# Loads on ACT's queue, one row of shifts and another order of the last heads, in a one-core hybrid decoder step

## The chip, the core and the metric

The kernel runs on one core of a Trainium2 chip. The core has five engines that run on their own and wait for one another through semaphores: TensorE (PE) multiplies matrices into PSUM, VectorE (DVE), ScalarE (ACT) and GpSimd (POOL) work on rows, and SyncE (SP) here only issues transfers (DMAs). ACT and POOL can issue transfers too. The metric is the device time of one execution in microseconds; lower is better.

## What is computed

One layer of a decoder for a prompt of 2048 positions and for 8 decode rows of one position each, with 512 cached positions per row. All data is float32.

- `h = rms_norm(x)`, then one product `p = h @ w_in` (1024 to 3592 columns), split into q, k, v, the forget gate, `za`, `u`, `gv`, `zc`.
- Attention, 8 heads of 64: q and k are RMS-normed, the logit of query t and key s is `q.k * SCALE + c_t - c_s` with `c` the running sum of `log_sigmoid(fz + b_f)`, under a causal mask; then softmax and the sum over v.
- A gating group: `gv` normed, multiplied inside chunks of 128 positions by a lower triangular matrix, plus a bias, times `u`.
- `y = x + concat(attn * silu(za), mix * u * silu(zc)) @ w_out`. Keys, values, log gates and the normed `gv` of the decode rows are outputs too.

The decode rows do the same with keys, values and gates gathered from pages of a cache by `page_table`.

## The kernel before

For precision each factor is split into two parts that TensorE takes at full rate, so a product is three matmuls (hi x hi, hi x lo, lo x hi).

**Order.** TensorE's instructions stay in the order in which the program writes them. The other engines' are ordered by a planner, which simulates the time line and takes what is ready first. The kernel keeps its own clock of TensorE's work (`Pe.clock`, from a number of nanoseconds given with each matmul). `later(ns, fn)` puts a piece of work off until that clock has moved on by `ns`; what it then writes may not be planned ahead of the last matmul written. `pump()` runs what is due. At the end of the program each instruction on SP in the attention stage is tied in the same way to the last matmul written before it. Instructions that ACT issues are not part of that last tie.

**Stage 1** (to about 590 us): `order` runs through eight units of columns of `w_in`. For units 3, 0, 1, 2 (q, k, v, gate) and 4 (`gv`) each of the 16 tiles of 128 positions is one product of 24 matmuls into a bank `acc` (four banks). Units 5, 6 and 7 (`u`, `zc`, `za`) work with features on the partitions and do only the first two chunks of 512 positions (`cp` 0 and 1); the rest is left as filler. `sample_products` multiplies the decode rows with a unit's weights; it joins tile 14 (`NT - 2`), or the last group of `cp` 1. Weights are loaded by `load_unit` (L291) and split by ACT or POOL and by DVE (L253 to L256). From tile 8 of unit 4 on, `decode_scores` loads the cached keys, 32 pages of 256 KB.

**Stage 2** (to about 1175 us): attention. `UNITS` lists 32 units (head, chunk of 512 queries), a unit of chunk c having 4c+4 key tiles. `values` does for each key tile two score matmuls into a bank `sc` (three banks), an exponential on ACT (L991) into one of ten ring tiles, and the row sums' addition on POOL (L1000); the sums over v (`av`) run after each eight key tiles. Two key tiles `k1` (hi and lo) and `k2` (hi and rows for gates and shifts) and the values `vst` belong to a head; `load_keys` and `load_values` load them on SP (L852, L853; L861, L862, L864). `load_queries` (L882 to L886) loads the next unit's queries in five transfers, `QLEAD` = 6 key tiles before the unit's end.

The exponential needs a shift per query, so `maxima` computes all scores once more, some 0.8 heads ahead, with DVE reducing each bank (`tp`, three banks) to a minimum (L925, L927). `shifts` turns four columns of minima into two rows (hi and lo, L942, L943), which are transposed, copied by ACT (L949) and stored to `mrow` (L953); `load_queries` brings them back as rows 66 and 67 of the queries.

After a unit its weighted values `at` (L1012 to L1014) are stored to `aT`, the reciprocal row sums (L1021 to L1031) to `rT`. After an odd head `gate` loads both heads' rows, `z` and the sums (L1080 to L1083), multiplies them and stores to `gm`. When the last pair of heads has finished a chunk, its four tiles can go through the output product: `out_inputs` loads a tile (L1101, L1102), ACT and DVE split it, `out_products` multiplies by `w_out`, whose sixteen blocks `load_out_weights` brings (L1067).

**Fillers.** `fill(ns)` writes matmuls of the remaining `u`, `zc`, `za` work, then of the output product, into the gaps, at `FILL` = 0.5 of the attention's own clock (0.95 in the last three units). What is left of the output product runs alone at the end (stage 3). `decode_attention` runs beside the attention from head 1 on: gates summed by one scan (L684), then for each of 8 rows four pages of cached values into a tile `vb` (L643), a product and a store.

**Places.** Large tiles (8 KB a partition) share 16 places: normed rows of both remaining chunks 8, ring tiles 2, `k1` and `k2`, `keep`, `vb`, later output weights. Small ones (`s2`, 2 KB a partition) share 11.

Of the kernel before, what the change touches and what calls it, by code (L numbers as in the profile page):

```python
# [9 lines left out]
F32 = mybir.dt.float32  # L10
F32R = mybir.dt.float32r
# [8 lines left out]
P = 128  # L20
# [4 lines left out]
NH = 8  # L25
# [37 lines left out]
WOENG = ('act',)  # L63
# [15 lines left out]
def hymba_step(ctx, tc, x_prompt, x_sample, cache_k, cache_v, cache_logf, page_table, g_norm, w_in,  # L79
# [45 lines left out]
    def s2(dt=F32, t="s2"):  # L125
        return wk.tile([P, 512], dt, tag="t2", name=tname(t))

# [102 lines left out]
    mrow = dr.tile([NH, 2, SEQ], F32, name="mrow")  # L230
# [436 lines left out]
    def decode_attention():  # L667
# [16 lines left out]
        nc.vector.tensor_tensor_scan(cc, one, lfT, 0.0, op0=ALU.mult, op1=ALU.add)  # L684
# [23 lines left out]
        for b in range(B):  # L708
            hs = slice(b * NH, (b + 1) * NH)
            vb = s8(t="vb").rearrange("p (g f) -> p g f", g=NPG)  # L710
            page_loads(b, range(NPG), [(cv, lambda g: vb[:, g])])
# [12 lines left out]
            yield DEC[2]  # L724
# [122 lines left out]

    def load_keys(h):

        k2 = s8(F32R, "k2")  # L850
        b = 512 + h * HD
        nc.sync.dma_start(k2[:HD].bitcast(F32), qk_hi[b:b + HD])  # L852
        nc.sync.dma_start(k2[HD:HD + 4].bitcast(F32), kx[h])  # L853
        return dict(h=h, k2=k2)

    def load_values(hd):
# [17 lines left out]
    def load_queries(h, c):  # L874
# [11 lines left out]
        nc.sync.dma_start(t[HD + 2:HD + 4, 512:].bitcast(F32), mrow[h, :, cs])  # L886
# [10 lines left out]
    def maxima(hd):  # L897

        h = hd["h"]
        nxt = qhi.pop() if qhi else load_hi(h, 0)  # L900
        for c in range(2):
            q = nxt
            for i in range(8 * c, 8 * c + 8, 2):
                if i == 2:
                    nxt = load_hi(h, 1)
                if i == 10 and h + 1 < NH:
                    qhi.append(load_hi(h + 1, 0))
                if i % 4 == 0:
                    part = sm.tile([P, 4, i // 4 + 1], F32, tag="mn", bufs=3, name=tname("mn"))
                cuts = [pieces((j + 1) * P) for j in (i, i + 1)]  # L910
                ends = []
                for j, cut in zip((i, i + 1), (cuts[0], cuts[1][::-1])):
                    for (c0, m) in cut:
                        n = cuts[j - i].index((c0, m))
                        end = n == len(cut) - 1
                        sp = bank("tp")[:, :m]
                        mm(sp, q[:HD + 2, (j % 8) * P:(j % 8 + 1) * P], hd["k2"][:HD + 2, c0:c0 + m], True, not end,
                           max(m, 256) * 0.422)
                        if end:
                            ends.append((sp, m, j, n))  # L920
                            if j > i:
                                for (sp, m_, _, _) in ends:
                                    mm(sp[:, m_ - P:], identb, maskb[:, 0], False, True, 56)
                                for (sp, _, j_, n_) in ends:
                                    nc.vector.tensor_reduce(part[:, j_ % 4, n_:n_ + 1], sp, axis=AX.X, op=ALU.min)  # L925
                        else:
                            nc.vector.tensor_reduce(part[:, j % 4, n:n + 1], sp, axis=AX.X, op=ALU.min)  # L927
                        yield m * 0.422
                if i % 4 == 2:
                    shifts(h, i // 4, part)  # L930
# [404 lines left out]
```

## Time and profile before

| | |
|---|---|
| median of 3 runs (lowest to highest) | 1345.62 us (1344.01 to 1347.55) |
| the profiled execution's own time | 1351.46 us |
| its span | 1349.7 us |
| PE busy in the span | 1304.4 us, 97% |
| DVE / POOL / ACT busy | 675.7 / 618.0 / 443.2 us |
| bytes moved | 183.10 MB |
| mean granted TensorE clock | 0.983 |

Busy time counts instructions being worked on; waiting, and the issue of transfers, is not busy. A granted clock of 1.00 is full speed. A wait row names the engine and line that waited, what ended the wait, the total, the count and the longest. A timeline row has start and duration in us, engine, line, operation, output and inputs, and in brackets the idle time before it and what ended that. `SPq` is SP's queue issuing a transfer.

### The profile page before, as it was taken

How to read it: one execution, taken by the hardware profiler on the slowest of the kernel's cores; microseconds unless marked ns; L12 is line 12 of the kernel's file. 1: busy time of each engine (PE TensorE's matmuls, PEld its weight loads, DVE VectorE, ACT ScalarE, POOL GpSimd, SP SyncE). 2: the span in 40 equal slices, each digit the busy share in tenths (PEclk: the TensorE clock that was granted, in tenths of full speed). 3: DMA queues.
4: the chain of work that ended last, by engine and by line, in shares of the span. 5: the costliest groups of instructions: out<-in, count | busy, mean ns of one | idle time of the engine just before them, and what ended most of it. 6: DMA issues, size and time to landing. Idle time of an engine off the chain costs nothing.

```text
span 1349.7 us, 19517 instructions
## 1 busy us (share of the span) xinstructions
PE 1304.4 (97%) x6544; PEld 1012.9 (75%) x6544; DVE 675.7 (50%) x1280; ACT 443.2 (33%) x805; POOL 618.0 (46%) x703
## 2 busy tenths in 40 slices
PE   6999999999999999999999999999999998999998
PEld 5999999999887877866666566656656664688877
DVE  4346654534678454264486453454455675222321
ACT  5542332322222111114454343534454455310000
POOL 3113343423223464317777666686769668600000
PEclk9999999999999999989999899998999998999999
DMA  6644354545113655534343845466374745573321
GB/s 216 187 120 111 86 141 120 156 133 158 51 50 106 190 176 156 159 81 127 77 116 112 190 124 140 133 176 177 91 201 113 189 126 174 167 245 116 108 76 50
DMA packets 170807, 183.10 MB, mean 136 GB/s; under 512 B 39403, under 2 KB 125867, under 8 KB 169139
## 3 DMA queue, kind: packets, MB, share of 16 engines
q1 hardware_dynamic: 166818, 173.08, 46.5%
q10 hardware_dynamic: 3488, 8.39, 1.6%
q8 instruction: 52, 0.85, 0.3%
q14 instruction: 49, 0.39, 0.1%
q0 software_dynamic: 400, 0.38, 0.1%
HBM read 121.53 MB, written 60.28 MB: 135 GB/s over the span
## 4 chain that ended last, share of the span: by engine, by line
PE 86%; DMA 5%; DVE 4%; issue 2%; SPq 2%; ACT 1%; POOL 0%; DVEq 0%; ACTq 0%; POOLq 0%
PE acc L174 35%; PE sc L174 21%; PE fl L174 10%; PE av L174 8%; PE tp L174 6%; PE tp L178 4%; DMA q<-qk_hi 2%; PE pm L174 1%; DMA xp<-in_x_prompt_dram 1%; DVE wl L256 1%; DVE mn L925 1%; DMA vb<-in_cache_v_dram 1%; DMA kb<-in_cache_k_dram 1%; SPq L641 0%; SPq L291 0%
## 5 line engine op out<-in xcount | busy, mean ns | idle before, releaser
L1000 POOL TENSOR_TENSOR acc<-acc,p 128x512 f32<-128x512 f32 (+3 forms) x256 | 284.9, 1113 | 61.8 <-ACT p L991 48.4
L991 ACT ACTIVATE p<-sc,zero 128x512 f32<-128x512 f32 (+1 forms) x320 | 194.9, 623 | 179.9 <-PE sc L174 175.0
L174 PE MATMUL acc<-wh,hh 128*128 128x384 f32 (+2 forms) x640 | 228.8, 357 | 0.0
L174 PE MATMUL acc<-wl,hh 128*128 128x384 f32 (+2 forms) x640 | 222.8, 348 | 0.8 <-DVE wl L256 0.8
L174 PE MATMUL acc<-wh,hl 128*128 128x384 f32 (+2 forms) x640 | 222.5, 348 | 0.6 <-DVE hl L248 0.6
L174 PE MATMUL sc<-q,k 128*128 128x512 f32 (+7 forms) x640 | 202.7, 398 | 11.9 <-DMA q<-qk_hi 10.5
L174 PE MATMUL sc<-wo,am 128*128 128x512 f32 x720 | 164.3, 390 | 0.0
L174 PEld LDWEIGHTS sc<-wo,am 128*128 128x128 f32 x720 | 134.9, 188 | 28.2
L927 DVE TENSOR_REDUCE mn<-tp 128x1 f32<-128x320 f32 (+5 forms) x192 | 118.4, 631 | 59.4 <-PE tp L174 58.0
L174 PEld LDWEIGHTS sc<-q,k 128*128 128x128 f32 (+1 forms) x640 | 120.0, 197 | 31.9 <-issue 13.8
L174 PE MATMUL av<-p,vst 128*64 128x512 f32 (+3 forms) x640 | 136.6, 547 | 0.0
L236 POOL TENSOR_SCALAR sm<-sm 128x6 f32<-128x6 f32 (+3 forms) x84 | 20.7, 246 | 238.5 <-DVE sm L389 170.5
L174 PE MATMUL tp<-k,q 66*128 66x384 f32 (+6 forms) x320 | 122.6, 398 | 6.2 <-DVE mn L925 2.4
L174 PEld LDWEIGHTS acc<-wh,hh 128*128 128x128 f32 x640 | 120.6, 188 | 7.4 <-POOL wh L255 0.3
L174 PEld LDWEIGHTS acc<-wl,hh 128*128 128x128 f32 x640 | 120.7, 189 | 6.2 <-DVE wl L256 1.6
L174 PEld LDWEIGHTS acc<-wh,hl 128*128 128x128 f32 x640 | 120.4, 188 | 6.3 <-DVE hl L248 1.1
L174 PEld LDWEIGHTS av<-p,vst 128*64 128x64 f32 x640 | 48.5, 138 | 67.6 <-issue 58.0
L925 DVE TENSOR_REDUCE mn<-tp 128x1 f32<-128x512 f32 (+7 forms) x128 | 66.8, 561 | 56.5 <-PE tp L174 56.3
L237 POOL TENSOR_TENSOR sm<-sm,mhalf 128x6 f32<-128x6 f32 (+3 forms) x84 | 89.5, 1066 | 6.7
L174 PEld LDWEIGHTS tp<-k,q 66*128 66x128 f32 x320 | 61.8, 194 | 32.7 <-DVE mn L925 5.7
L174 PE MATMUL acc<-hh,wh 128*128 128x512 f32 x192 | 76.3, 397 | 4.6 <-DVE s L378 4.6
L998 POOL TENSOR_TENSOR acc<-p 128x512 f32<-128x512 f32 x32 | 40.9, 1278 | 85.5 <-ACT p L991 75.3
(213 smaller groups left out, 1967.6 us busy)
## 6 DMA issues: line engine op xcount, KB each, us to landing
raw<-in_w_in_dram SPq DMA_DIRECT2D x40, 256.0 KB
kb<-in_cache_k_dram SPq DMA_DIRECT2D x32, 256.0 KB
k<-qk_hi SPq DMA_DIRECT2D x16, 512.0 KB
q<-qk_hi SPq DMA_DIRECT2D x64, 128.0 KB
vb<-in_cache_v_dram SPq DMA_DIRECT2D x32, 256.0 KB
g<-gm SPq DMA_DIRECT2D x16, 512.0 KB
xy<-in_x_prompt_dram SPq DMA_DIRECT2D x16, 512.0 KB
out_dram<-xy ACTq DMA_DIRECT2D x15, 512.0 KB
```

Of the source, the lines that this page charges most:

```text
L174: Pe.last = nc.tensor.matmul(out, lhsT, rhs, start=start, stop=stop).ins
L178: Pe.last = nc.tensor.transpose(out, in_, idn).ins
L236: nc.gpsimd.tensor_scalar(r, ss, inv_n, EPS, op0=ALU.mult, op1=ALU.add)
L237: nc.gpsimd.tensor_tensor(r, r, mhalf[:rows, :n], op=ALU.pow)
L256: nc.vector.scalar_tensor_tensor(lo, src, g, hi.bitcast(F32), op0=ALU.mult, op1=ALU.subtract)
L925: nc.vector.tensor_reduce(part[:, j_ % 4, n_:n_ + 1], sp, axis=AX.X, op=ALU.min)
L927: nc.vector.tensor_reduce(part[:, j % 4, n:n + 1], sp, axis=AX.X, op=ALU.min)
L991: nc.scalar.activation(p[:, n0:], sp[:, n0:], AF.Exp, bias=zero1, scale=-1.0)
L998: nc.gpsimd.tensor_tensor(acc, p0, p, op=ALU.add)
L1000: nc.gpsimd.tensor_tensor(acc[:, n0:], acc[:, n0:], p[:, n0:], op=ALU.add)
```

## The change

- **Queues.** `load_keys` and `load_values` issue through ACT's queue (`big_load`). `k2` has 67 rows in place of 68.
- **Shifts.** `shifts` transposes the minima as they are; ACT's copy negates and rounds them; `mrow` has one row, stored in one transfer.
- **Places.** `four_rows` gives the transposed shifts and row sums places in a constant tile of their own.
- **Decode rows.** `sample_products` joins tile 11 and, in units 5 to 7, the last group of `cp` 0. The scan goes in four pieces; cached values are loaded a page at a time, 3250 ns of clock apart, a row each 13000 in place of 26000.
- **Queries.** `QLEAD` is 10 where the next unit's shifts are there, else 4.
- **Last heads.** Units of heads 6 and 7 alternate from (7, 0) on; `maxima` goes by units in that order; keys of head 7 are loaded at unit (5, 2), values at (6, 1).
- **Gate.** An odd head's weighted values stay in SBUF; the gate's inputs are loaded earlier, its lags are shorter.
- **Output.** Output weights are loaded three at a time, each next one after a split. The product runs in halves: tiles 0 and 1 with the first half of the weights, then with the second. The dense filling starts with the last four units.
- **Start.** 64 bf16 matmuls on a constant run before the first tile.

```diff
-WOLAG = 9000.0
+WOLAG = 7000.0
-GTLAG = 8000.0
+GTLAG = 4000.0
+OLAG0 = 5000.0
+RTLAG = 1500.0
+NDENSE = 4
+WARM = 64
+SAT = 11
-UNITS = [(h, c) for h in range(6) for c in range(4)] + [(6, 0), (6, 1), (6, 2), (7, 0), (6, 3), (7, 1), (7, 2), (7, 3)]
+UNITS = [(h, c) for h in range(6) for c in range(4)] + [(6, 0), (6, 1), (7, 0), (6, 2), (7, 1), (6, 3), (7, 2), (7, 3)]
-QLEAD = 6
+QLEAD = 10
-DEC = (3300, 15000, 26000, 14000)
+DEC = (3300, 15000, 13000, 12000)
...
+    rows = const.tile([P, 2, P], F32, name="rows")
+    nrow = [0]
+
+    def four_rows():
+
+        n = nrow[0] % 8
+        nrow[0] += 1
+        return rows[32 * (n % 4):32 * (n % 4) + 4, n // 4]
...
-        nc.vector.tensor_tensor_scan(cc, one, lfT, 0.0, op0=ALU.mult, op1=ALU.add)
+        for g in range(NPG):
+            gs_ = slice(g * P, (g + 1) * P)
+            nc.vector.tensor_tensor_scan(cc[:, gs_], one[:, gs_], lfT[:, gs_], cc[:, g * P - 1:g * P] if g else 0.0,
+                                         op0=ALU.mult, op1=ALU.add)
+            yield 1500
...
-            page_loads(b, range(NPG), [(cv, lambda g: vb[:, g])])
+            for g in range(NPG):
+                page_loads(b, (g,), [(cv, lambda g: vb[:, g])])
+                if g < NPG - 1:
+                    yield DEC[2] / NPG
...
-            yield DEC[2]
+            yield DEC[2] / NPG
...
+    def big_load(dst, src):
+        nc.scalar.dma_start(dst, src)
...
-        nc.sync.dma_start(k2[:HD].bitcast(F32), qk_hi[b:b + HD])
-        nc.sync.dma_start(k2[HD:HD + 4].bitcast(F32), kx[h])
+        big_load(k2[:HD].bitcast(F32), qk_hi[b:b + HD])
+        big_load(k2[HD:HD + 3].bitcast(F32), kx[h, :3])
...
-        nc.sync.dma_start(k1[:HD].bitcast(F32), qk_hi[b:b + HD])
-        nc.sync.dma_start(k1[HD:].bitcast(F32), qk_lo[b:b + HD])
+        big_load(k1[:HD].bitcast(F32), qk_hi[b:b + HD])
+        big_load(k1[HD:].bitcast(F32), qk_lo[b:b + HD])
...
-        nc.sync.dma_start(vst, v_st[h])
+        big_load(vst, v_st[h])
...
-        mx = sm.tile([P, 2, 4], F32R, tag="mx", bufs=2, name=tname("mx"))
...
-        nc.vector.tensor_scalar(mx[:, 0], m4, -1.0, None, op0=ALU.mult)
-        nc.vector.scalar_tensor_tensor(mx[:, 1], m4, -1.0, mx[:, 0].bitcast(F32), op0=ALU.mult, op1=ALU.subtract)
...
-            transpose(pt[:8, :P], mx.rearrange("p r n -> p (r n)").bitcast(F32), ident)
-            t = s2(t="mt")[:8, :P]
-            nc.scalar.copy(t, pt[:8, :P])
+            transpose(pt[:4, :P], m4, ident)
+            t = four_rows()
+            nc.scalar.activation(t.bitcast(F32R), pt[:4, :P], AF.Copy, scale=-1.0)
...
-                for r in range(2):
-                    nc.sync.dma_start(mrow[h, r, c * 512:(c + 1) * 512].rearrange("(n p) -> n p", p=P), t[4 * r:4 * r + 4])
+                nc.sync.dma_start(mrow[h, c * 512:(c + 1) * 512].rearrange("(n p) -> n p", p=P), t)
...
-            if kt == max(0, 4 * c + 4 - QLEAD) and at + 1 < len(UNITS):
+            if at + 1 < len(UNITS) and UNITS[at + 1] not in qload and kt >= 4 * c + 4 - (
+                    QLEAD if UNITS[at + 1] in shifted else 4):
                 qload[UNITS[at + 1]] = load_queries(*UNITS[at + 1])
...
-                    t = s2(t="at")
-                    nc.scalar.copy(t[:HD], av[HD:])
-                    nc.vector.tensor_tensor(t[:HD], t[:HD], av[:HD], op=ALU.add)
-                    later(STLAG if h < NH - 2 else STLAST, lambda: nc.sync.dma_start(aT[h * HD:(h + 1) * HD, c * 512:(c + 1) * 512], t[:HD]))
+                    if h % 2 == 0:
+                        t = s2(t="at")
+                        nc.scalar.copy(t[:HD], av[HD:])
+                        nc.vector.tensor_tensor(t[:HD], t[:HD], av[:HD], op=ALU.add)
+                        later(STLAG, lambda: nc.sync.dma_start(aT[h * HD:(h + 1) * HD, c * 512:(c + 1) * 512], t[:HD]))
+                    else:
+                        t = s2(t="ga")
+                        nc.scalar.copy(t[HD:], av[:HD])
+                        nc.vector.tensor_tensor(t[HD:], t[HD:], av[HD:], op=ALU.add)
...
             def parts():
-                split(hi, lo, raw, WOENG[n % len(WOENG)])
+                split(hi, lo, raw, "act")
                 wo_hl[k, f] = hi, lo
+                if n + 3 < KT:
+                    load(n + 3, KORDER[n + 3])
             later(WOLAG, parts)
-        for n, k in enumerate(KORDER):
-            later(n * WOSTEP, lambda n=n, k=k: load(n, k))
+        for n in range(3):
+            later(n * WOSTEP, lambda n=n: load(n, KORDER[n]))
...
-        later(OLAG, parts)
+        later(OLAG if i >= OFIRST else OLAG0, parts)
...
-        for i in range(NT):
-            while i not in ins or not ins[i] or len(wo_hl) < 2 * KT:
+        halves = [(0, 0), (1, 0), (0, 1), (1, 1)] + [(i, f) for i in range(2, NT) for f in range(2)]
+        for n, (i, f) in enumerate(halves):
+            while i not in ins or not ins[i] or (KORDER[-1], f) not in wo_hl:
...
+        warm = bank("pm", P)
+        for _ in range(WARM):
+            mm(warm, identb, identb, True, True, 0)
...
-                    if i == NT - 2:
+                    if i == SAT:
                         group.insert(0, sample_products(unit, WID[u], SEGS[u]))
...
-                        if cp == NCP - 1 and f == 1:
+                        if cp == 0 and f == 1:
                             group.insert(0, sample_products(unit, WID[u], SEGS[u]))
...
-        if c == 0 and h < NH - 1:
-            heads[h + 1] = load_keys(h + 1)
+        if c == 0 and h < NH - 2 or (h, c) == (NH - 3, 2):
+            heads[len(heads)] = load_keys(len(heads))
+        if (h, c) == (NH - 2, 1):
+            load_values(heads[NH - 1])
...
-        dose = FILL if at < len(UNITS) - 3 else FILL7
+        dose = FILL if at < len(UNITS) - NDENSE else FILL7
```

More of the change, by code (lines that the diff above doesn't have):

```diff
@@ L62 @@
 KORDER = (4, 5, 6, 7, 0, 1, 2, 3)
-WOENG = ('act',)
 OFIRST = 2
@@ L895, in load_hi @@
         return t
[L897 to L930, printed above, removed]
@@ L1048, in all_maxima @@
     def all_maxima():
-        for h in range(NH):
-            yield from maxima(heads[h])
-            if h + 1 < NH:
-                load_values(heads[h + 1])
+        for n, (h, c) in enumerate(UNITS):
+            ahead = UNITS[n + 1][0] if n + 1 < len(UNITS) else 0
+            yield from maxima(h, c, ahead)
+            if "k1" not in heads[ahead] and ahead < NH - 1:
+                load_values(heads[ahead])
     wo_hl = {}
```

103 lines of the change are left out of this document (68 added, 35 removed).

## The prediction, made before the result was known

> **What bounds the kernel now.** I read the page first, then the waits of TensorE (PE), then a table of stretches of 25 us, then the timeline of the queues around each gap.
>
> ```profile
> span 1349.7 us, 19517 instructions
> PE 1304.4 (97%) x6544; PEld 1012.9 (75%) x6544; DVE 675.7 (50%) x1280; ACT 443.2 (33%) x805; POOL 618.0 (46%) x703
> PEclk9999999999999999989999899998999998999999
> ```
>
> PE works 97% of the span, so there are only 1349.7 - 1304.4 = 45.3 us of idle time to win, about 10 of them at the start and 3 or 4 at the end. The clock row is the second loss: it dips in six slices, and a busy PE at half clock counts as busy. The waits of PE (sum, times, longest) and the stretches in which the clock dips (length, then busy time and count of PE, PEld, DVE, ACT, POOL, then granted clock, DMA share, GB/s):
>
> ```profile
> PE sc L174 <- DMA q<-qk_hi: 10.5, 3, 4.8
> PE acc L174 <- DVE s L378: 4.6, 3, 2.4
> PE tp L178 <- DVE mx L943: 3.0, 2, 1.8
> PE tp L174 <- DVE mn L925: 2.4, 6, 1.1
> PE fl L174 <- DVE sz L490: 1.8, 2, 1.4
> PE sc L174 <- ACT p L991: 1.5, 3, 0.8
> ```
> ```profile
> 425.00:450.00 25.00, 22.58 (x98) 17.71 (x97) 17.12 (x32) 5.37 (x8) 11.95 (x13) 0.93 0.70 188
> 575.00:600.00 25.00, 22.67 (x94) 16.25 (x94) 13.79 (x29) 3.08 (x6) 3.39 (x7) 0.86 0.33 88
> 725.00:750.00 25.00, 24.94 (x111) 16.14 (x112) 18.41 (x32) 10.77 (x20) 20.32 (x21) 0.93 0.42 98
> 750.00:775.00 25.00, 22.22 (x105) 14.46 (x104) 12.27 (x21) 9.47 (x19) 15.48 (x20) 0.86 0.92 231
> 825.00:850.00 25.00, 23.60 (x120) 15.11 (x116) 9.95 (x22) 9.62 (x18) 15.07 (x18) 0.93 0.73 191
> 900.00:925.00 25.00, 21.73 (x103) 14.17 (x98) 9.53 (x22) 8.27 (x15) 13.15 (x13) 0.86 0.91 217
> 1100.00:1125.00 25.00, 23.84 (x102) 12.51 (x102) 16.82 (x24) 15.62 (x29) 22.54 (x19) 0.89 0.45 137
> 1125.00:1150.00 25.00, 19.87 (x83) 11.38 (x82) 10.89 (x12) 14.06 (x25) 19.26 (x17) 0.84 0.66 210
> ```
>
> Each stretch shows a short stall and then a lost share of clock. 25 us times (1 - clock) is 1.75, 3.5, 1.75, 3.5, 1.75, 3.5, 2.75 and 4.0 us: 22.5 us, as much as the waits listed (23.8 us). Part of it falls into the idle time and is counted twice; I keep that as the margin. So a stall of 1 to 5 us costs 3 to 9.
>
> **The change part by part.** No part takes PE work away worth naming (one row less in a matmul, 68 to 67, changes no column count), so its worth is which of these stalls go.
>
> *Sample products in mid-unit* (SAT, and cp 0). The sum of the decode rows' product held an accumulator bank while DVE finished weight splits ahead of it:
>
> ```profile
> 435.76 0.75 DVE L256 SCALAR_TENSOR_TENSOR wl<-raw,gT,wh 128x512 fp32r<-128x512 f32 x1
> 436.43 0.67 DVE L378 TENSOR_TENSOR s<-s,acc 8x512 f32<-8x512 f32 x1
> ```
>
> At tile 11 three more tiles run before the unit ends, and at cp 0 the splits of the next unit aren't issued yet. The 4.6 us of waits go, and 1.75 of clock at 425: 6.35, I take 6; at least 4.6 if the clock dips for another reason.
>
> *Shifts in one row.* This removes L942 and L943 from every unit (columns: busy, mean ns, idle):
>
> ```profile
> L942 DVE TENSOR_SCALAR mx<-sm 128x4 fp32r<-128x4 f32 x23 | 15.8, 687 | 0.4
> L943 DVE SCALAR_TENSOR_TENSOR mx<-sm,mx 128x4 fp32r<-128x4 f32 x23 | 8.6, 373 | 0.7
> 686.34 3.29 DVE L942 TENSOR_SCALAR mx<-sm 128x4 fp32r<-128x4 f32 x1
> ```
>
> About 1.06 us on DVE per unit, and one of these four-column operations took 3.29 us. The negation moves into the ACT copy that is there anyway, and one store per unit goes. The 3.0 us of PE waits go; with them, if nothing is late just behind, 3.5 of clock at 575. Between 3.0 and 6.5 I take 5. The own places for sums and shifts free work buffers; the small waits on them are below 2 us in all, I take 1.
>
> *Scan in four pieces.* One scan held DVE while PE wanted its score banks back:
>
> ```profile
> 722.69 1.80 DVE L684 TENSOR_TENSOR_SCAN cc<-one,lfT 64x512 f32<-64x512 f32 x1 [2.87 <-ACT lfT L683]
> ```
>
> The longest PE wait on L925 (1.1), a neighbour of 0.2 and 1.75 of clock make 3.1; a quarter of 1.80 is 0.45, which one free bank covers. I take 2.9, and 1.1 at least. The dip after so short a wait is the trace's (0.93 in its stretch). The Trainium skill, "TensorE: Matmul & The Clock Gate", on oscillation, has the clock fall only after idle gaps of some 3.4 us; the stretches at 725 (0.06 idle, and 1.4 just before) and 825 (1.40) speak against it. By the rule the sum would be smaller by 1.75 + 1.75 + 3.5, about 7 us, since those dips would not hang on the stalls.
>
> *Key and value loads on ACT's queue, queries at ten key tiles before the end, cached values one page at a time.* The stall at 911:
>
> ```profile
> 896.77 4.43 SPq L643 DMA_DIRECT2D vb<-in_cache_v_dram  x4
> 901.31 0.47 SPq L852 DMA_DIRECT2D k<-qk_hi  x1
> 904.07 0.52 SPq L853 DMA_DIRECT2D k<-kx  x1
> 904.68 0.44 SPq L882 DMA_DIRECT2D q<-qk_hi  x1
> 910.31 0.23 SPq L886 DMA_DIRECT2D q<-mrow  x1
> SPq L884 <- DMA k<-qk_hi: 1.6, 1, 1.6
> 911.61 1.19 PE L174 MATMUL sc<-q,k 128*128 128x512 f32 x2 [2.97 <-DMA q<-qk_hi]
> ```
>
> Four cached pages, then keys, then the five query loads in one queue; the queries begin 8 us late and PE meets them. SP loses two key issues here (0.47 + 0.52) and the wait of 1.6 behind them. But a unit with c = 0 has four key tiles, so its successor's queries can't start earlier than now: 10 or 6 tiles of lead are both all of it. The stalls at 755 (22.22 busy: 2.8 idle, 3.5 clock) and 911 (3.0 and 3.5) are of that kind; I take 3 of 6.3 and 4 of 6.5. The third, 4.8 us at 1145, is a unit of 12 tiles whose successor is asked for at tile 6, behind out-tile inputs; at tile 2 it comes four tiles earlier. The stage from 600 to 1175 has 320 key tiles, so four are some 7 us against 4.8 late. Of 4.8 + 4.0 I take 7. Sum 14, bounds 0 and 21.6. At 836 PE waited for L490 (1.4 and 1.75 of clock) because DVE had waited for such pages:
>
> ```profile
> 833.66 0.68 DVE L1013 TENSOR_TENSOR at<-at,av 64x512 f32<-64x512 f32 x1 [1.65 <-DMA vb<-in_cache_v_dram]
> ```
>
> I take 2 of 3.15.
>
> *What the moved loads cost.* 40 issues at about 0.5 us are 20 us of ACT's queue in front of its exponentials. Cover: ACT idles for most of each key tile.
>
> ```profile
> L991 ACT ACTIVATE p<-sc,zero 128x512 f32<-128x512 f32 x224 | 152.2, 688 | 145.3 <-PE sc L174 141.5 <-POOL gz L1086 1.2 <-PE tp L178 0.7
> SPq L852 <- PE sc L174: 4.7, 1, 4.7
> ACT wo L243 <- DMA raw<-in_w_out_dram: 6.1, 5, 2.1
> ```
>
> 575 us over 320 tiles is 1.8 us a tile, with 0.69 of exponential; three score banks let PE run about 5 us ahead. A load that waits for its place now stops ACT, not SP; the longest such wait so far was 4.7. I charge 2, from 0 to 8 heads x 5.
>
> *Decode rows at twice the rate* (DEC 13000 for 26000): the same 32 loads in half the time, so fewer heads meet them and those meet more. I charge 2, bounds 0 and one stall of 6.5.
>
> *Last heads interleaved, output weights in a chain of three, first out tiles by halves, shorter lags, NDENSE.* Chunk 0 finishes a 12-tile unit earlier, so out products cover the stretch 1100 to 1150 in which PE had none to mix in and waited for ACT (1.5 in all, with 2.75 of clock). The work only moves from behind the loop into it: without a stall to cover it is worth nothing. ACT waited 6.1 us for raw output weights, and the lag there shrinks (9000 to 7000). Of 4.2 I take 2, bounds -2 and 4.2.
>
> *Warming matmuls.*
>
> ```profile
> 1.66 0.30 DVE L190 CAST identb<-ident 128x128 bf16<-128x128 f32 x1 [0.72 <-POOL ident masks.py:199]
> 9.98 1.97 PE L178 MATMUL tp<-ident,xp 128*128 128x128 f32 x8 [9.98 <-DVE xp L308]
> 14.40 1.03 PE L178 MATMUL tp<-ident,xp 128*128 128x128 f32 x8
> 22.81 1.07 PE L178 MATMUL tp<-ident,xp 128*128 128x128 f32 x8 [1.24 <-DVE fz_all L445]
> ```
>
> They fit between 2.0 and 9.98 and can save the 0.94 us by which the first eight transposes are slow, and about as much in the next matmuls; PE then waits at 22.81 anyway, for 1.24. I take 0, from -1.9 to +1.
>
> **The sum.** 6 + 5 + 1 + 2.9 + 14 + 2 + 2 = 32.9 off, 2 + 2 on: 28.9 us less. Against the profiled execution's 1351.46 that is 1322.6; the median shown, 1345.62, is 5.84 below that execution, so I forecast 1345.6 - 28.9, about **1317**. With every stall gone, (6.35 + 6.5 + 2 + 3.1 + 21.6 + 3.15 + 4.2 + 1.9) = 48.8 less, hence 1297; with the low takes about 1329.
>
> **The rivals.**
> *Transfers, not issues, are late* (18%). At 750 and 900 the DMA share is 0.92 and 0.91, and the keys' bytes stay the same. Then 755 gains its issue time of 1, 911 gains 2.6, 1145 gains 3: 6.6 in place of 14, so 1324. Against it: at 911 PE started 1.1 us after the last query issue, so issuing was the late part there. This would also be the Trainium skill's rule ("DMA: Bandwidth & Descriptors", on issuing engines not being separate queues), by which another engine's queue saves only issue time.
> *The places run out* (18%). Of 16 big tiles, 8 hold normed rows, 2 probabilities, 4 keys of two heads, 1 the decode scores: one is left for cached values, which now live longer (three quarter steps and 12000) than a row's 13000. The next row waits for its place and its four pages come in one burst again, twice as often. Term 14 falls to 0 and one stall of 6.5 comes on top: 1345.6 - 28.9 + 20.5 = 1337. For it: the count; against it: a burst is late only where a short unit follows.
> *ACT stops behind its loads* (12%), the slower side. The place is the head's first unit: the key load waits for a place or an earlier transfer, exponentials stand behind it, PE runs out of banks. From a wait of about 5 us on, each head pays the rest and a dip of some 3.5 us. At 3.6 us a head (8 heads) the gain is gone; a wait of 6.5 us pays 5 a head, 40 in all: 1345.6 - 28.9 + 40 = 1357. Against it: 4.7 was the longest.
> *Gain and such waits cancel* (5%): within 4 us of before, 1346.
>
> **How the numbers follow.** The forecast has 47%. About 0.3%, 4 us, is what a measurement can tell from no change. Forecast, first and second rival are faster: 0.83; the last 0.05 the same; the third 0.12 slower. The range leaves out the slow rival, the cancelling one and the outermost tail where all stalls go: 1301 to 1342.
>
> **What would show it.** No wait of PE on L378, none on a shift operation; DVE busy down by some 24 us; no gap over 1 us near the decode scan; waits on q well under 10.5 us; PEclk without dips before slice 16; ACT's idle before exponentials put down to PE, not to its own loads. I am wrong if PE's idle time stays near 45 us or if exponentials wait for key loads.

## The result: 1.2% slower, and the profile after

The kernel after takes 1361.93 us (median of 4 runs, 1356.81 to 1362.2), the kernel before, run beside it, 1344.82 (1342.53 to 1347.55): a ratio of 1.0117, with a 95% interval from 1.0086 to 1.0148. The forecast was 1317 in a range of 1301 to 1342, with 12% for slower. It was wrong in sign.

The profiled execution of after is its fastest one, 1356.81 us. Against the 1351.46 of before the two traces differ by 5.4 us, a third of what the medians differ by; so sizes are taken below from timed comparisons, and the traces show places.

From the page of the kernel after: span, busy times, granted clock.

```profile
span 1354.8 us, 19483 instructions
PE 1305.3 (96%) x6608; PEld 1011.1 (75%) x6608; DVE 652.6 (48%) x1219; ACT 444.4 (33%) x805; POOL 615.3 (45%) x703
PEclk9999999999999999999999999998998999999999
```

DVE gave up the 23 us that the change takes from it (675.7 to 652.6), and PE still idles for 49.5 us of its span, against 45.3 before. The warming matmuls count as busy here:

```profile
2.02 5.68 PE L187 MATMUL pm<-identb 128*128 128x128 bf16 x64 [2.02 <-DVE identb L203]
```

Without these 5.7 us, which do none of the layer's work, PE's idle time is 55.2 us, 9.9 more than before. PE's waits in the kernel after (sum, times, longest):

```profile
PE fl L187 <- DVE sz L503: 4.9, 5, 2.4
PE tp L187 <- ACT rows L1052: 4.8, 1, 4.8
PE sc L187 <- issue: 4.5, 1, 4.5
PE sc L187 <- DMA q<-mrow: 3.7, 2, 3.2
```

Of the rows of before, the wait on the sample rows' sum and that on DVE's shift operation (L943) are gone, and `q<-qk_hi` fell from 10.5 to 0.7 us. Others stand in their place, some of them on queries too: 3.7 us on `q<-mrow`, 4.5 under "issue", where the profile shows nothing that PE waited for (they are the first queries, below), and 1.7 on the maxima's queries (`q<-kx`), with the 0.7 some 10.6 us in all. Their stretches, in the columns of the forecast's table (length; busy time and count of PE, PEld, DVE, ACT, POOL; clock; DMA share; GB/s):

```profile
600.00:625.00 25.00, 19.56 (x81) 13.58 (x82) 8.88 (x17) 7.74 (x14) 10.21 (x12) 0.80 0.51 124
925.00:950.00 25.00, 20.15 (x87) 12.36 (x85) 8.01 (x16) 9.01 (x16) 17.15 (x19) 0.86 0.60 166
975.00:1000.00 25.00, 21.83 (x106) 14.87 (x105) 10.01 (x18) 10.52 (x19) 15.95 (x20) 0.93 0.59 145
1000.00:1025.00 25.00, 22.87 (x104) 12.85 (x103) 10.61 (x21) 11.68 (x21) 17.91 (x19) 0.86 0.30 85
```

In these four PE idles for 15.6 us and loses 13.75 us of clock by the forecast's 25 x (1 - clock).

*At 602 the first queries are late.* SP's queue in the kernel after (start, duration), then the matmul that waited:

```profile
594.47 0.27 SPq L971 DMA_DIRECT2D mrow<-rows  x1
601.57 0.35 SPq L532 DMA_DIRECT2D zT<-sz  x1
602.03 0.46 SPq L905 DMA_DIRECT2D q<-qk_hi  x1
```
```profile
606.59 0.77 PE L187 MATMUL sc<-q,k 128*128 128x512 f32 x1 [4.49 <-issue]
```

SP stood for 7 us before a store whose data were not there yet; behind it were the first unit's queries. In the kernel before they had gone out at 594.35, ahead of that store.

*At 982 SP waits for transfers that ACT issued.* The two longest waits of SP's queue between 980 and 998 in the kernel after:

```profile
SPq L532 <- DVE sz L503: 10.4, 1, 10.4
SPq L907 <- DMA k<-qk_hi: 4.8, 1, 4.8
```

The first is again a zT store, gone out at 981.35, just ahead of these queries; L907 loads queries, and L906 and L905 wait there for loads of k too (2.2 and 1.5 us). These loads of k are all on ACT's queue. The 3.2 us on `q<-mrow` are the stall that follows. The store alone doesn't make it: with the loads on SP's queue (the first run below) SP waits 13.2 us for the same store and this stall is gone. The 4.8 us at 930 hang on a late weight load: POOL waited 8.0 us for it, ACT 6.9 for POOL, and the copy that PE needed stood behind ACT's cast.

### The profile page after: what moved, and what is told of

Read it like the earlier page. It is cut to its first block, busy times and chain, and to the rows that moved or that the text cites. A ratio compares the mean times of both kernels' runs of the same rounds, so it can differ in the third digit from the quotient of the medians.

```text
span 1354.8 us, 19483 instructions
## 1 busy us (share of the span) xinstructions
PE 1305.3 (96%) x6608; PEld 1011.1 (75%) x6608; DVE 652.6 (48%) x1219; ACT 444.4 (33%) x805; POOL 615.3 (45%) x703
## 4 chain that ended last, share of the span: by engine, by line
PE 79%; DMA 7%; DVE 5%; POOL 3%; issue 3%; ACT 2%; SPq 1%; ACTq 0%; POOLq 0%; DVEq 0%
PE acc L187 32%; PE sc L187 20%; PE fl L187 11%; PE av L187 8%; PE tp L187 5%; PE tp L191 3%; DMA raw<-in_w_in_dram 1%; PE pm L187 1%; POOL acc L1019 1%; DMA xp<-in_x_prompt_dram 1%; POOL sm L250 1%; DMA q<-mrow 1%; ACT p L1010 1%; DVE wl L269 1%; DVE mn L948 1%
## 5 line engine op out<-in xcount | busy, mean ns | idle before, releaser
L187 PE MATMUL sc<-q,k 67*128 67x512 f32 (+7 forms) x640 | 202.7, 396 | 9.4 <-issue 4.5
L187 PE MATMUL sc<-wo,am 128*128 128x512 f32 x624 | 142.7, 390 | 0.0
L187 PEld LDWEIGHTS sc<-wo,am 128*128 128x128 f32 x624 | 116.8, 188 | 24.8 <-PE av L187 0.4
L187 PE MATMUL fl<-hh,fh 128*128 128x512 f32 x176 | 74.4, 423 | 5.0 <-DVE sz L503 4.9
```

Source lines behind the costliest of these rows:

```text
L187: Pe.last = nc.tensor.matmul(out, lhsT, rhs, start=start, stop=stop).ins
```

## The experiments

The ratio is always to the kernel before, run on the same chip beside it, with its 95% interval.

**Key and value loads back on SP, in the kernel after.**

```diff
-        nc.scalar.dma_start(dst, src)
+        nc.sync.dma_start(dst, src)
```

> The changed kernel with its key and value loads issued by SP again; everything else as changed. Theory A (a load issued by ACT still holds SP's queue, since SP's query loads were seen to wait 4.8 us for such a load to complete, and ACT's issues come at times of their own): about 1355 us, 7 less than the changed kernel's 1362, and the wait of PE on queries at the first unit of a late head shrinks. Rival B (the loss is not in the queue but in the order that the planner gave the other transfers): within 4 us of 1362.

1357.89 us, ratio 1.0067 [1.0036, 1.0098], 4.0 us less than after by the medians, 7 by the ratios, which is between the two expectations. The stall at 992 is gone; one of 4.5 us at 603 (the first queries) is left and one of 3.9 stands at 937. ACT's queue is a part of the loss here, but a small one.

**The last heads in the old order, in the kernel after.**

```diff
-... [(6, 0), (6, 1), (7, 0), (6, 2), (7, 1), (6, 3), (7, 2), (7, 3)]
+... [(6, 0), (6, 1), (6, 2), (7, 0), (6, 3), (7, 1), (7, 2), (7, 3)]
```

> The changed kernel with the last heads in the order of before (7,0 after 6,2). Theory C (interleaving the last heads costs, since three query halves and both heads' keys press for places and out products start early): about 1350 us. Rival: the loss lies ahead of 1080 us and this order only moves work between the loop and the end: within 4 us of 1362.

1349.76 us, ratio 1.0038 [1.0017, 1.0059]: the new order of the last units costs about 12 us by the medians, 11 by the ratios.

**Only the parts local to DVE, on the kernel before**: sample products in mid-unit, shifts in one row, own places for sums and shifts, the scan in pieces.

```diff
+SAT = 11
...
-        nc.vector.tensor_tensor_scan(cc, one, lfT, 0.0, op0=ALU.mult, op1=ALU.add)
+        for g in range(NPG):
...
+            t = four_rows()
+            nc.scalar.activation(t.bitcast(F32R), pt[:4, :P], AF.Copy, scale=-1.0)
```

> The kernel before with only the parts that take work from DVE or move it: sample products in mid-unit, shifts in one row, own places, scan in four pieces. The prediction's terms for these are 6 + 5 + 1 + 2.9: about 1330 us. Rival: a stall removed here lets PE run into the next one (queries), so that under half arrives: 1338 to 1346 us.

1344.58 us, ratio 0.9985 [0.9963, 1.0007]: no difference that can be told, as the rival had it. The waits on L378 and on the shift operation at 589 (L943) are gone, but PE waits 5.9 us at 604 for the first queries, and 3.1 at 732 beside the decode scan. The moves had let that zT store slip in front of them, as in the kernel after.

**Only ACT's queue, on the kernel before.** All five loads of a head, nothing else; TensorE's order is the same.

```diff
-        nc.sync.dma_start(k2[:HD].bitcast(F32), qk_hi[b:b + HD])
+        nc.scalar.dma_start(k2[:HD].bitcast(F32), qk_hi[b:b + HD])
...
-        nc.sync.dma_start(vst, v_st[h])
+        nc.scalar.dma_start(vst, v_st[h])
```

> The kernel before with only the key and value loads moved to ACT's queue; TensorE's order is the same. Prediction's terms: query stalls at 755 and 911 lose 7 us, 2 us are paid: about 1340 us. Theory A: no gain, 1345 to 1352 us, with SP's query loads still waiting for key loads. The slower rival of the prediction (ACT stops behind its loads) would show 1350 or more with ACT's exponentials waiting for key loads.

1361.23 us, ratio 1.0129 [1.0092, 1.0166]: this part alone costs as much as the whole change, more than the theory had, and no exponential waits for a key load. ACT's queue in this run, then SP's waits around it, then the matmul that waited:

```profile
898.19 0.49 ACTq L852 DMA_DIRECT2D k<-qk_hi  x1
899.26 0.49 ACTq L861 DMA_DIRECT2D k<-qk_hi  x1
899.79 0.61 ACTq L862 DMA_DIRECT2D k<-qk_lo  x1
```
```profile
SPq L1081 <- DMA k<-qk_hi: 4.5, 1, 4.5
SPq L883 <- DMA k<-qk_lo: 2.7, 1, 2.7
SPq L882 <- DMA k<-qk_hi: 1.8, 1, 1.8
```
```profile
917.35 1.39 PE L174 MATMUL sc<-q,k 128*128 128x512 f32 x2 [8.99 <-DMA q<-qk_hi]
```

In the kernel before only the keys (901 and 904) went out ahead of the five query loads, the last of which is L886 at 910.31, and L861 and L862 came behind them:

```profile
911.14 0.59 SPq L861 DMA_DIRECT2D k<-qk_hi  x1
```

Here all but the last go out in one burst before. SP's query issues (L882, L883) wait until loads of that burst have landed, and PE waits 9.0 us. The order of before had come from the last lines of the program, which hold each of SP's issues behind the TensorE instruction ahead of it; they name SP only, so a load on ACT goes as soon as its place is free.

**The same loads on ACT's queue, held in order.** The last loop takes them in too.

```diff
+        act_loads.add(nc.scalar.dma_start(dst, src).ins.name)
...
-        elif i.engine == mybir.EngineType.SP and last is not None:
+        elif (i.engine == mybir.EngineType.SP or i.name in act_loads) and last is not None:
```

> The kernel before with the loads of keys and values on ACT's queue, as in the run on ACT's queue alone (1361 us, ratio 1.0129), but each of these loads is now given a place behind the TensorE matmul that stands ahead of it in the program, as SP's loads have it. Theory (the loads ran ahead of the queries because nothing held them back, and SP's query issues then waited for them): with the order restored the 9 us stall at 908 shrinks below 4 us, no query issue of SP waits over 2 us for a load of k, and the time is 1342 to 1352 us, ratio 0.997 to 1.005. Rival (the second queue itself costs, by its bytes on the shared DMA engines or by ACT's time): the stalls at 908 and 993 stay and the time is 1356 us or more, ratio 1.008 or above.

1351.72 us, ratio 1.0027 [1.0012, 1.0042]: some 10 us come back by the medians, 14 by the ratios, with the same queue and the same bytes. The free order was the larger part. The details held less well (the profiled execution is the slowest of its ten, 1357.98 us): the stall of 908 is still 3.7 us, the one of 1140 is 5.8, and SP's query issues still wait for loads of k, at the maxima up to 2.6 us and at one unit's second query load (L888) 12.0 us. SP's wait there, and ACT's load:

```profile
SPq L888 <- DMA k<-qk_hi: 12.0, 1, 12.0
```
```profile
605.01 0.45 ACTq L851 DMA_DIRECT2D k<-qk_hi  x1
```

SP had issued the load ahead of L888 at 597.70 and issued L888 at 610.14. ACT issued no load of k between 555.92 and 605.01, so for seven of the twelve us SP stood before a transfer that ACT hadn't issued yet. So ACT's queue in order is still no better than SP's.

**The first queries early, in the kernel after.**

```diff
+        if UNITS[0] in shifted and UNITS[0] not in qload:
+            qload[UNITS[0]] = load_queries(*UNITS[0])
```

> The kernel after, with the first unit's queries loaded as soon as its shifts are stored, ahead of the zT store that SP waits for from 594 to 601 us. Theory (that place in SP's order makes the 4.5 us stall at 602 and the clock of 0.80 behind it): the stall goes, the stretch from 600 to 625 has a granted clock of 0.95 or more, and the time is 5 to 8 us below the kernel after: 1354 to 1357 us, ratio to before 1.005 to 1.009. Rival (PE waits there for something else that is late at the same moment, the bank of a sum or the values): a stall of 3 us or more stays between 595 and 615 and the time stays within 2 us of 1362.

1354.43 us, ratio 1.0051 [1.0034, 1.0068], 7.5 us less than after (9 by the ratios), as the theory has it. In its stretch from 600 to 625 PE is now busy for 24.54 us in place of 19.56, and the clock is 1.00 in place of 0.80.

**Three of these together, and the local parts with early queries.** The first is the kernel after with SP's queue, the old heads and the early first queries; the second is the run of the local parts with the early first queries. Their edits are those above.

> The kernel after with three parts changed at once: key and value loads back on SP's queue, the units of the last heads in the order of before, the first unit's queries early. Theory (the three losses stand side by side and add): 1362 less 4, less 12, less 6 makes 1340 us, ratio 0.993 to 0.998. Rival (a stall removed only moves to the next late transfer): 1346 to 1350 us, ratio 1.000 to 1.004.

> The kernel before with only the parts local to DVE (sample products in mid-unit, shifts in one row, own places, scan in four pieces), which alone gave 1344.6 us, plus the first unit's queries early. Theory (the forecast's gain of the local parts, some 14 us, was given back at the first queries, 5.9 us and a dip of the clock, and at stalls that remain at 449, 586, 713 and 732): 6 to 8 us below, 1337 to 1339 us, ratio 0.993 to 0.995. Rival (the gain is lost again right behind, because the next late transfer takes the stall): 1343 us or more, ratio 0.998 or above.

1340.9 us, ratio 0.9926 [0.9899, 0.9953], and 1338.66 us, ratio 0.9932 [0.9908, 0.9956]. Both theories hold: the three losses add, and the local parts do gain once the queries are not behind the store. Also, all else that after has (lead, single pages, gates, halves of out tiles, warming) brings nothing that shows between these two.

**The earlier call alone and the single pages alone, on the kernel before.**

```diff
-            if kt == max(0, 4 * c + 4 - QLEAD) and at + 1 < len(UNITS):
+            if at + 1 < len(UNITS) and UNITS[at + 1] not in qload and kt >= 4 * c + 4 - (
+                    QLEAD if UNITS[at + 1] in shifted else 4):
```
```diff
-            page_loads(b, range(NPG), [(cv, lambda g: vb[:, g])])
+            for g in range(NPG):
+                page_loads(b, (g,), [(cv, lambda g: vb[:, g])])
+                if g < NPG - 1:
+                    yield DEC[2] / NPG
```

> The kernel before with only the earlier call for the next unit's queries (up to ten key tiles ahead instead of six, where the shifts are stored). The order on TensorE stays as it was; only SP's order changes. The forecast's step: the stall of 4.8 us at 1140 goes with its 4 us of clock, those at 755 and 908 stay, since units with four key tiles can't be called earlier: 1338 to 1342 us, ratio 0.993 to 0.997. Rival (the queries are late because SP stands behind other transfers, not because they are called late): the stall at 1140 stays above 3 us and the time is within 2 us of before, ratio 0.998 or above.

> The kernel before with only the cached values one page at a time, at double the rate of the decode steps. The forecast's step: four pages no longer stand ahead of the keys and queries at 897, so the stall at 908 falls below 1.5 us and that at 834 goes: 1340 to 1343 us, ratio 0.995 to 0.998, whatever the double rate costs being under 2 us. Rival (other transfers hold SP at the same moments, and the double rate brings the decode's work of ACT, DVE and POOL closer together): a stall of 3 us or more between 880 and 1000 and a time of 1346 us or more, ratio 0.999 or above.

The lead: 1343.17 us, ratio 0.9977 [0.9958, 0.9996], 3.7 us less, between its two expectations. The pages: 1351.48 us, ratio 1.0025 [1.0008, 1.0042], 4.6 us more. PE's waits in the lead's run, then in the pages' run:

```profile
PE sc L174 <- issue: 2.5, 1, 2.5
PE sc L174 <- DMA q<-qk_hi: 2.2, 1, 2.2
```
```profile
PE sc L174 <- DMA q<-qk_hi: 10.1, 4, 3.9
```

The lead took the 10.5 us on queries to 2.2 plus 2.5, and about two thirds of that shows in the time: a new 1.6 us stands at 1120 behind ACT's exponentials. Of the three stalls, the one of 4.8 is now 2.2 (at 1136), the one at 908 is 2.5 (at 902), and the one at 755, which the expectation had staying, is gone. The pages took the stall at 908 from 3.0 to 1.9, but that at 755 grew from 2.7 to 3.9 and one of 1.2 came at 836: the bytes met other queries, as the rival had it, though the new stalls aren't where it said.

**Both on the run of the local parts with early queries**: the lead alone, then lead and pages.

> The run of the local parts with the first queries early (1338.7 us, ratio 0.9932) plus the earlier call for queries. There no wait of 1 us on queries is left behind 985, so the theory (the lead wins only what still stalls) gives 1336 to 1341 us, ratio 0.991 to 0.996, within 2 us of that run. Rival (the lead brings queries ahead of something that PE needs sooner): 1342 us or more.

> The run of the local parts with the first queries early (1338.7 us) plus the earlier call and the single pages at double rate: all of the change but ACT's queue, the interleaved last heads and the small moves in the gates, the output weights and the warming. Theory (the parts of the change that were left in the run of 1340.9 us cost nothing): 1336 to 1342 us, ratio 0.991 to 0.996. Rival (the single pages remove the 5.3 us wait at 923, where the late load of weights stands behind four pages): 1330 to 1335 us, ratio 0.988 to 0.991.

1335.43 us, ratio 0.9902 [0.9869, 0.9934], and 1337.01 us, ratio 0.9926 [0.9898, 0.9953]. The first is the fastest kernel of this study, ahead of before and after. The intervals overlap, so whether the pages cost here too isn't settled. With them the wait at 923 falls below 1.6 us as the rival expected, but 3.5 us appear at 938, and its time isn't reached.

**Order against queue inside the kernel after**: early first queries, and ACT's loads held in order; then the same on SP's queue.

> The kernel after with the first queries early (1354.4 us, ratio 1.0051) and, besides, its key and value loads on ACT's queue given a place behind the TensorE matmul ahead of them in the program. Theory (what ACT's queue costs in the kernel after is the order too): the waits of SP's query issues for loads of k around 985 fall below 2 us, the stall at 991 goes, and the time is 1347 to 1352 us, ratio 1.000 to 1.004. Rival (in the kernel after the order costs nothing; what it lost against SP's queue, 4 us, is the second queue's own): 1353 us or more, ratio 1.0045 or above.

> The kernel after with the first queries early and its loads on SP's queue: the run of 1340.9 us but for the interleaved last heads. Theory (interleaving the last heads costs by itself, 10 to 12 us, by stalls on late queries and out-tile inputs between 1010 and 1130): 1349 to 1354 us, ratio 1.002 to 1.006. Rival (the heads cost only where the queries were late for another reason, which is now gone): 1341 to 1345 us, ratio 0.993 to 0.998.

1349.72 us, ratio 1.0016 [1.0003, 1.0028], and 1351.37 us, ratio 1.0033 [1.0009, 1.0057]. In order, ACT's queue is no slower than SP's. The waits of query issues at 985 and the stall at 991 are gone, but 5.7 us stand at 1009, at the maxima's queries. The second run differs from the one of 1340.9 us only in the order of the last units: 10.5 us by the medians, 14 by the ratios, so interleaving costs by itself. The stretch from 1000 in the run with the old heads, then in this run, then this run's longest SP wait from 985 to 1012 and its stalled matmul:

```profile
1000.00:1025.00 25.00, 24.56 (x129) 15.53 (x126) 13.98 (x28) 14.64 (x26) 20.52 (x24) 1.00 0.58 145
```
```profile
1000.00:1025.00 25.00, 19.98 (x87) 10.94 (x87) 9.92 (x21) 10.42 (x19) 16.88 (x21) 0.80 0.39 97
```
```profile
SPq L532 <- DVE sz L503: 8.1, 1, 8.1
```
```profile
1008.96 0.66 PE L187 MATMUL tp<-k,q 66*128 66x384 f32 x1 [3.11 <-DMA q<-kx]
```

SP again stands before a zT store, for 8.1 us; behind it are a row store, keys, queries and the maxima's next half. 4.6 us more of PE's time and 5 us of clock go in this stretch. The store can't be the whole of it: the run with the old heads has the same wait, with the same issues behind it, and its stretch from 1000 is at 1.00. SP's wait there from 985 to 1012, then in this run SP's call for the maxima's half:

```profile
SPq L532 <- DVE sz L503: 6.9, 1, 6.9
```
```profile
1004.78 0.45 SPq L916 DMA_DIRECT2D q<-qk_hi  x1
```

PE wanted that half at 1005.85, 1.1 us after this call. The store had gone out ten us earlier, at 995.10, and what SP waited for ahead of L916 was TensorE (`SPq L916 <- PE tp`, 0.5 us): the call came late by the program. `maxima` calls for the next half after two tiles of a unit, and in the new order the half that (6, 2) begins with is called for inside (7, 0), a unit of four tiles; in the old order it's called for in (6, 0). All five runs with interleaved heads have a wait of PE on the maxima's `q<-kx`, from 1.7 to 5.7 us, and no run with the old order has one. The 1.4 us at 1002, ahead of the stall shown, are on the first maxima of head 7, whose keys went out at 997.39, behind the store; so the store may have made that part. How much of the 10 to 14 us is the late call isn't shown: no run called earlier.

**The fastest kernel with its loads on ACT's queue in free order.** Edit as in the run of ACT's queue alone.

> The fastest kernel so far (local parts, first queries early, earlier call; 1335.4 us, ratio 0.9902) with its key and value loads on ACT's queue in their free order, nothing else. Theory (the free order costs what it did in the kernel before, where the queries stand behind the burst of loads): 1345 us or more, ratio 0.997 or above, with a stall of 4 us or more on q near 900 or 985. Rival (with ten key tiles of lead the queries are ahead of the burst, and it costs what it did between the kernel after on ACT's and on SP's queue): 1336 to 1341 us, ratio 0.990 to 0.995.

1362.55 us, ratio 1.0104 [1.007, 1.0138]: 27 us more than the same program on SP's queue, TensorE's order being the same. The rival falls: a lead of ten tiles doesn't protect the queries. One head start, first in the fastest kernel (SP's queue, then the stalled matmul), then in this run (ACT's queue, SP's queue, the stalled matmul):

```profile
965.13 4.11 SPq L653 DMA_DIRECT2D vb<-in_cache_v_dram  x4
970.47 0.45 SPq L896 DMA_DIRECT2D q<-qk_hi  x1
977.45 0.45 SPq L875 DMA_DIRECT2D k<-qk_hi  x1
```
```profile
976.50 1.55 PE L184 MATMUL sc<-q,k 128*128 128x512 f32 x2 [2.65 <-DMA q<-qk_hi]
```
```profile
988.55 0.45 ACTq L875 DMA_DIRECT2D k<-qk_hi  x1
989.04 0.61 ACTq L876 DMA_DIRECT2D k<-qk_lo  x1
```
```profile
987.21 4.84 SPq L653 DMA_DIRECT2D vb<-in_cache_v_dram  x4
993.94 0.46 SPq L896 DMA_DIRECT2D q<-qk_hi  x1
```
```profile
1003.62 1.40 PE L184 MATMUL sc<-q,k 128*128 128x512 f32 x2 [7.76 <-DMA q<-qk_hi]
```

Within one queue the queries (L896) went 1.2 us after the pages and 7 us before the loads that a later tile needs (L875). With two queues the 1 MB of L875 and L876 goes out beside the pages, and the first query issue comes 1.9 us behind the pages, the last (L900, at 998.54) 4.6 us after it.

## Why the prediction was wrong, step by step

The runs as a ladder, each with one step more than the one above; the last is the kernel after. The medians come from several chips, so the ratios are what to compare:

| from the kernel before | median, us | ratio |
|---|---|---|
| local parts, first queries early | 1338.66 | 0.9932 |
| + earlier call for queries | 1335.43 | 0.9902 |
| + single pages at double rate | 1337.01 | 0.9926 |
| + gates, output weights, halves, warming and the rest | 1340.9 | 0.9926 |
| + interleaved last heads | 1351.37 | 1.0033 |
| + ACT's queue, free order | 1354.43 | 1.0051 |
| first queries behind the zT store | 1361.93 | 1.0117 |

*The step that failed first* is the charge of 2 for the moved loads, and with it the term of 14. I costed the 40 issues as time on ACT, and asked only what stands behind them there. ACT hardly waits for them; its longest wait on a load of k in the kernel after:

```profile
ACT p L1010 <- DMA k<-kx: 0.6, 1, 0.6
```

What I left out is what kept these loads in their place on SP. Off SP they overtake the queries, and SP's issues wait for them. On the kernel before that costs 1.29%, some 17 us (14 by the medians), on the fastest 27 us; in the kernel after, where the heads and the first queries lose at the same time, only 3 to 4 of it show by the medians, 2 to 7 by the ratios. The slower rival had the right part and its time (1357) came close, but its mechanism, exponentials behind the loads, didn't make the loss: in the runs with ACT's free order the longest wait of an exponential on a load of k is 2.2 us. Of "Transfers, not issues, are late" the premise held. The Trainium skill ("DMA: Bandwidth & Descriptors", section "Issuing engines are not separate DMA queues") has all such transfers on the same engines, so that a second issuer saves only its issue time; no run here tests the first half, and on the second they show that it isn't a floor: a second issuer can also lose 14 to 27 us.

*The lead* was worth 3.7 us alone and 3.2 on top of the local parts (4 by the ratios, whose intervals overlap), for the 7 taken. The mechanism was right in part: the stall of 4.8 us fell to 2.2, so the term was oversized, and ACT is late next; but the stall at 755, which I said a longer lead couldn't reach, went. *The single pages*, which shared the takes of 3 and 4 with the moved loads and were booked at 2 less 2 besides, cost 4.6 alone.

*The local terms* (6, 5, 1 and 2.9) sum to 14.9; measured are 9 us (0.9932). The waits on L378 went as said. The scan's term failed otherwise than by its pieces. PE's longest wait beside it fell from 1.1 to 0.2 us in the kernel after, though the four pieces took 5.6 us there, three times the one scan; in the run of the local parts with early queries it rose to 1.6, behind a product of the gate on DVE. A quarter of 1.80 us is what a piece takes only where it doesn't stand behind one of POOL's additions, as the last section shows. Among PE's waits in the fastest kernel is this one:

```profile
PE tp L188 <- DVE mx L952: 1.7, 1, 1.7
```

It is still a shift operation (the minimum over parts, L952), which I had said would leave no wait.

*The last heads*, booked as a gain of 2 with a lower bound of -2, cost 10 to 14. I weighed only PE's cover, and neither SP's queue, past which the units and their maxima move, nor how long before its use the new order calls for the maxima's next half. *The first queries* aren't in the prediction at all: with the local parts a store slipped ahead of them, as the run of these parts alone shows, and 7.5 us went (1354.43 against 1361.93; 9 by the ratios). *The places run out* wasn't seen: the pages in the kernel after go out singly.

Of the signs named, the waits on L378, DVE's 23 us, the small gap near the scan and ACT's waits came as said, and PE's idle time near 45 us said that I was wrong. The clock before slice 16 told nothing: the page of before has its first dip in slice 18. The waits on q were 6.1 us by their rows, but 10.6 with the first queries' wait, which stands under "issue". The signs that came tell of the stalls that were removed; only PE's idle time sees what came in their place.

Two figures of the prediction are off without bearing on its step: the clock row of before dips in four slices, not six, and the lower bounds given with the terms (4.6, 3.0, 1.1, 0 and -2) and the two takes without bounds (1 and 2) sum to 9.7, hence about 1336 before any cost, not 1329.

What stays open: how much of interleaving's 10 to 14 us the late call makes, whether the single pages cost anything beside the other parts, and the 4.8 us at 930, which no run removed alone in the kernel after.

## What to carry to other kernels

Before a load is moved to another queue, find out what orders it on the old one; a queue that is in nobody's way also lets big transfers start ahead of small urgent ones, and the first queue can be made to wait until they have landed. Where one in-order queue carries stores that wait for data and loads that are due soon, each small shift of the schedule can put the one before the other, so pin the urgent load to its cause. When units change places, look at how far ahead of its use each load is called for in the new order. Time the parts of a bundled change one by one: here 12 us of gain stood beside more than 20 us of loss.

## What the runs showed of the hardware

*SP waits for the transfer eight issues back.* SP's waits in the kernel before between 895 and 912, then the issues that stand between those of the forecast's fence:

```profile
SPq L883 <- DMA vb<-in_cache_v_dram: 0.6, 1, 0.6
SPq L885 <- DMA gz<-zT: 0.6, 1, 0.6
SPq L886 <- DMA ga<-aT: 1.1, 1, 1.1
```
```profile
901.88 0.53 SPq L1080 DMA_DIRECT2D gz<-zT  x1
902.46 0.42 SPq L1081 DMA_DIRECT2D ga<-aT  x1
902.93 1.09 SPq L1083 DMA_DIRECT2D gr<-rT  x2
```

None of these is data that a query load needs. Counted back along the queue, the issues of the forecast's fence put in between (L852 ahead of these, L853 and L882 behind), each names the issue eight places earlier, and so does the wait of L884 on L852's transfer. In the runs on ACT's queue SP waits in the same way for loads that ACT issued. So big transfers hold up the small ones issued behind them, and a second queue didn't lift that. That the limit is one for both queues is read off these waits, not tested; the wait of 12.0 us in the run with ACT's loads in order, most of it before ACT had issued the load, says the same, and that the count doesn't go by the time of issue.

*A piece of a scan is short where it doesn't stand behind POOL.* In the kernel after POOL's additions (1.35 us each) run back to back beside the pieces. In the run of the local parts alone the first piece falls into a pause of POOL (735.60 to 736.69):

```profile
734.46 6.75 POOL L1019 TENSOR_TENSOR acc<-acc,p 128x512 f32<-128x512 f32 x5
736.06 4.07 DVE L699 TENSOR_TENSOR_SCAN cc<-one,cc,lfT 64x128 f32<-64x128 f32 x3
```
```profile
736.00 0.42 DVE L696 TENSOR_TENSOR_SCAN cc<-one,lfT 64x128 f32<-64x128 f32 x1
```

Beside the additions a piece takes 1.36 us, the length of one of them; in the pause it takes 0.42, about a quarter of the 1.80 of 64x512. In the run of 1349.72 us the first piece takes 0.42 too; it starts at 723.91, with an addition and not behind one, and the next three take 4.06. That each piece waits for an addition to end is read off these rows, not tested.

*The clock can fall after a short wait.* In the run of 1340.9 us one wait of 1.84 us, 2.2 us idle in all, stands in a stretch at 0.86:

```profile
775.00:800.00 25.00, 22.76 (x94) 13.47 (x93) 10.10 (x17) 8.47 (x15) 15.97 (x16) 0.86 0.40 114
```
```profile
780.67 1.29 PE L187 MATMUL tp<-k,q 66*128 66x384 f32 x2 [1.84 <-DVE mn L948]
```

This is what the forecast took from the trace of before, against the 3.4 us of the Trainium skill's "TensorE: Matmul & The Clock Gate" (section on oscillation). It is no rule: in the kernel after a wait of 1.60 us, with as much idle time in all, left the stretch from 625 to 650 at 1.00.
